# Seven block products of eight for w_proj_b, the b gates through DRAM, and weight sums copied by ScalarE

## The chip, the cores and the metric

The kernel runs on one core of a Trainium2 chip. A core has five engines, each with its own queue of instructions: TensorE (PE, matrix products into PSUM), VectorE (DVE), ScalarE (ACT), GpSimd (POOL) and SyncE (SP, which here only issues DMAs). PE, DVE and ACT do the work; any of SP, ACT and POOL can issue a transfer, and transfers that add onto their target are issued by POOL. The metric is the time of one execution on the device in microseconds (us).

## The reference

The program is one encoder layer in float32 over 512 tokens of width 1024: two mixers side by side, then cross-attention to 256 memory tokens, then a SwiGLU feed-forward part (FFN).

```python
n = rms_norm(x); proj = n @ w_in                # columns: xa, zu, zv, gate_a, gate_b
ya = s5_branch(xa)                              # scans in both directions, GELU, GLU with w_glu
yb = gelu(zu) * (mix(layer_norm(gelu(zv))) + bias)
merged = gate_a * (ya @ w_proj_a) + gate_b * (yb @ w_proj_b)
h = x + merged @ w_out
h = h + attention(rms_norm(h), rms_norm(mem))   # w_q, w_k, w_v, w_xo
h = h + (silu(m @ w_gate) * (m @ w_up)) @ w_down     # m = rms_norm(h)
out = rms_norm(h)
```

The change lies at `yb @ w_proj_b`, a product of 512x1024 by 1024x1024, and at the gate that multiplies it.

## The kernel before, in words

**Number format.** Each operand of a product is split into a high half (`whi`, a cast on ACT, line 85) and a low half (`wlo`, the difference on DVE, line 86). A product is then three matmuls: high with high, high with low, low with high (`mm3`, line 314).

**The weight stream.** All weights pass through one list, `plan`, in the order of use. An entry is a block of 128x1024 numbers (512 KB). `next_w` hands out the next pair of halves. It starts the loads of entries up to three ahead (`LOADS`, issued by SP, line 124, tile `wraw`, three buffers) and the splits of entries up to two ahead (`SPLITS`). A block of `feat` is used for 24 matmuls of 512 columns.

**Order.** The rows of `w_in` come first: zv (first half), xa, zv (second half), the a gates, zu, the b gates. The layer norm of zv (lines 903 to 913) and the mixing run beside the a gates. The a gates are written to DRAM (`gad`, line 947) and read back into `gat` (line 1027) for use in `pa_evac`.

**The S5 branch beside it.** The S5 branch is a generator, `s5_program`. After each block, `tick` lets it go on for a share of the block's time and runs what `later` has put off. It has a setup, kernels for four octets of groups (`s5_kernels`, tiles `e`, `pk`, `kd`, `tt`), inputs (`zh`), a scan of 62 steps of four small DVE operations (lines 798 to 801), and outputs for each octet (`s5_outputs`: copies `ss` on ACT, matmuls `py` at lines 822 to 824, GELU into `y`, a store to DRAM `yd` at line 832). `finish_side` traces what is left of it; then its memory pool (`s5`) is closed and the pool `merge` is opened in its place (lines 995 to 999), beginning with a small `pad`, then `ygt` and `yg_hi`/`yg_lo`, the operand of w_glu.

**Who orders the instructions.** Each engine runs its queue in order. The order within a queue is set when the program is built: a list scheduler takes, for each engine, the earliest instruction of the program that it thinks is ready. `keep_in_program_order` pins one instruction behind everything that was traced before it on its engine.

**The part around the change (lines 983 to 995).** For each 256 output columns, two blocks of the b gates run, their sigmoid goes into `part`, then two blocks of w_proj_b run on `yb`, and DVE multiplies the result by the gate in place:

```python
    for c0 in range(0, D, 256):
        feat(w_in, OFF_GB + c0, xn, KD, gb_evac)
        feat(w_proj_b, c0, yb, KD, pb_evac)
```

**Sums of w_down in DRAM.** The FFN already uses a scheme of seven block products instead of eight (Winograd's form of Strassen's algorithm): `product` (line 1254) runs 24 matmuls of 256 columns for one of seven products `q`, whose operands are blocks or sums of blocks. For w_down, four sums of blocks are prepared in DRAM (`dsum`): a copy from DRAM to DRAM issued by SP (`start`, line 223) and, three plan entries later, an add on top of it issued by POOL (`add`, line 226). There are 24 copies and 24 adds, from plan entry 14 to entry 86.

Of the kernel before, what the change touches and what calls it, by code (L numbers as in the profile page):

```python
# [9 lines left out]
F32 = mybir.dt.float32  # L10
# [42 lines left out]
def hybrid_layer_kernel(  # L53
# [147 lines left out]

    DOWN, CHUNKS = (1, 5, 2, 6, 3, 7, 4), 6
    DSRC = {1: (0, 0), 2: (1, 0), 3: (1, 1)}
    dsum = {q: dp.tile([P, NF // 2, 512], F32, name=f"dsum{q}") for q in (4, 5, 6, 7)}

# [6 lines left out]

    def plan_sums(first, step):


        more = {5: lambda c: down_block(0, 1, c), 7: lambda c: down_block(1, 1, c),
                6: lambda c: down_sum(5, c), 4: lambda c: down_sum(6, c)}  # L220

        def start(q, i, jc, c):
            tc.keep_in_program_order(nc.sync.dma_start(down_sum(q, c), down_block(i, jc, c)))

        def add(q, c):
            nc.gpsimd.dma_start(down_sum(q, c), more[q](c), accum_op=ALU.add)

        j = first
        for q, i, jc in ((5, 0, 0), (7, 0, 1), (6, 1, 1), (4, 1, 0)):
            for c in range(CHUNKS):  # L230
                plan[j][1].append((0, lambda x=(q, i, jc, c): start(*x)))
                plan[j + step][1].append((0, lambda x=(q, c): add(*x)))
                j += step

    def plan_down(w, make_tokens, entries):
        for q in DOWN:
            for c in range(CHUNKS):
                got = {}

                def load(q=q, c=c, got=got):  # L240
                    src = down_block(*DSRC[q], c) if q in DSRC else down_sum(q, c)
# [12 lines left out]
    plan_tok(w_in, OFF_V + 512, KD)  # L254
    first_copy = len(plan)
    for c0 in range(0, D, 256):
# [25 lines left out]
    plan_units(UNITS, down_plan)  # L282
    plan_sums(first_copy + 2, 3)
    used_w = [0]
# [193 lines left out]
    def slot(tag, shape, dt, name):  # L478
        return sp.tile(list(shape), dt, tag=tag, name=name)

    def token_slot(name, shift=0):

# [43 lines left out]
    def s5_setup():  # L526
# [23 lines left out]
        for nm, src in (("br", s5_b_re), ("bi", s5_b_im), ("cr", s5_c_re), ("ci", s5_c_im)):  # L550
# [10 lines left out]
            for c in range(C):  # L561
                nc.tensor.transpose(ps[:, c, :], rows[:, :, c], ident[:G, :G])
            t = s5p.tile([P, G, C], F32, name="raw_" + nm)
            A_.copy(t, ps.rearrange("p c g -> p g c"))
# [45 lines left out]
        for src in (pr, pi):  # L610
            pe = s5p.tile([P, G, Q], F32, name="pe%d" % len(st["pe"]))
            pw = s5p.tile([P, G, Q], F32, name="pw%d" % len(st["pw"]))
            A_.copy(pe[lo_], src[lo_, :, 0:Q])
# [353 lines left out]

    yb_hi = slot("E", (P, KD, T), F32R, "yb_hi")
    yb_lo = slot("D", (P, KD, T), F32R, "yb_lo")
    yb = (yb_hi, yb_lo)  # L970

# [10 lines left out]

    part = slot("A", (P, KD, T), F32, "part")

    def gb_evac(m, j, ps):
        nc.scalar.activation(part[:, m - OFF_GB // P, :], ps, AF.Sigmoid)

    def pb_evac(m, j, ps):
        nc.vector.tensor_tensor(part[:, m, :], ps, part[:, m, :], ALU.mult)
# [240 lines left out]

    K0, K1, T0, T1 = slice(0, 4), slice(4, 8), slice(0, 256), slice(256, 512)
    a11, a12, a21, a22 = full[:, K0, T0], full[:, K1, T0], full[:, K0, T1], full[:, K1, T1]
# [19 lines left out]
    fn_q = lambda ks, ts: (fn_hi[:, ks, ts], fn_lo[:, ks, ts])  # L1252
    ops = {1: fn_q(K0, T0), 2: fn_q(K1, T0), 7: fn_q(K0, T1), 4: fn_q(K1, T1)}

    def product(ps, u, q, start):

        hi, lo = next_w(u[0], u[1], q)
        for j in range(2):
            cs = slice(j * P, (j + 1) * P)
            for k in range(4):  # L1260
                a = (hi[:, k, cs], lo[:, k, cs])
                b = (ops[q][0][:, k, :], ops[q][1][:, k, :])
                for i, (x, y) in enumerate(((0, 0), (0, 1), (1, 0))):
                    nc.tensor.matmul(ps[:, j, :], a[x], b[y], start=start and j == k == i == 0,  # L1264
                                     stop=k == 3 and i == 2, skip_group_check=True)
        tick(2.7)

    def unit_bank(name):
        return bank(name).rearrange("p (j t) -> p j t", j=2)

# [86 lines left out]
    for i, u in enumerate(UNITS):  # L1357
# [9 lines left out]
        product(x, u, 6, False)  # L1367
        u2 = stp[0].tile([P, 2, 256], F32, tag="u2", name="u2", bufs=2)
        u3 = np_.tile([P, 2, 256], F32, tag="ev", name="u3", bufs=2)
# [152 lines left out]
```

## Time and profile before

| | us |
|---|---|
| median of three runs | 917.19 |
| lowest and highest run | 914.25, 920.67 |
| the profiled execution's own time | 915.85 |
| span of the profiled execution, first to last instruction | 914.1 |

The busy times add up the instructions of each engine. The chain that ended last goes back from the last instruction, at each step to what released it. In a row of a timeline stand the start, the length, the engine, the line and the tiles; in brackets how long the engine was idle before and what released it. `SPq` and `ACTq` are DMA issues on those engines' queues. A row of windows has the stretch, its length, the busy time and number of instructions of PE, PEld (weight loads), DVE, ACT and POOL, then the granted clock of PE as a share of full speed, the share of the DMA engines and GB/s. In a group stand the count, the busy time and the mean ns of one, and then the idle time before them.

### The profile page before, as it was taken

The numbers are of one execution on the slowest core, as the hardware profiler recorded it, in microseconds if no ns is written. First come the engines' busy times: TensorE is split into PE (matmuls) and PEld (weight loads), VectorE is DVE, ScalarE is ACT, GpSimd is POOL, SyncE is SP. The second block draws the span as 40 slices with busy tenths as digits, with TensorE's granted clock in tenths as the row PEclk, the third lists the DMA queues.
The fourth block names the chain that finished last, engine by engine and source line by source line (L and its number), as shares of the span: only waits on it lengthen the run. The fifth ranks groups of instructions, "written<-read, shape, count | busy, mean of one in ns | idle before, by whom it ended". The sixth has DMA issues, their size and how long they took to land.

```text
span 914.1 us, 14130 instructions
## 1 busy us (share of the span) xinstructions
PE 897.4 (98%) x5510; PEld 789.2 (86%) x5510; DVE 609.0 (67%) x991; ACT 458.7 (50%) x671; POOL 109.1 (12%) x163
## 2 busy tenths in 40 slices
PE   7999999999999999999999999999999999999996
PEld 6888888888888887789998888999999999888875
DVE  5596662888753235868545444786778777899875
ACT  5542995244374333445434433655554555655663
POOL 3003210000025301502000001000000000000000
PEclk8999999999999999999999999999999999999999
DMA  8445263675546655686895217415456463246572
GB/s 269 127 120 151 85 164 126 181 205 133 141 138 158 144 185 156 216 260 191 244 291 147 71 68 233 113 65 142 119 154 144 118 160 94 70 147 207 188 241 82
DMA packets 105987, 142.77 MB, mean 156 GB/s; under 512 B 13232, under 2 KB 73152, under 8 KB 105920
## 3 DMA queue, kind: packets, MB, share of 16 engines
q1 hardware_dynamic: 90688, 120.14, 40.9%
q0 software_dynamic: 12064, 19.37, 12.9%
q10 hardware_dynamic: 3168, 2.36, 0.9%
q8 instruction: 43, 0.70, 0.3%
q14 instruction: 24, 0.20, 0.1%
HBM read 135.06 MB, written 29.85 MB: 180 GB/s over the span
## 4 chain that ended last, share of the span: by engine, by line
PE 86%; ACT 4%; DVE 4%; DMA 3%; issue 2%; POOL 1%; POOLq 0%; SPq 0%; ACTq 0%; DVEq 0%
PE pf L314 31%; PE pt L314 14%; PE px L1264 12%; PE pq L1264 6%; PE dx L314 5%; PE dq L314 3%; PE pv L1264 3%; PE dv L314 2%; PE pk L714 2%; DVE wlo L86 1%; PE ptr L466 1%; PE po L314 1%; PE psc L314 1%; DMA wraw<-dsum 1%; ACT whi L85 1%
## 5 line engine op out<-in xcount | busy, mean ns | idle before, releaser
L86 DVE TENSOR_TENSOR wlo<-wraw,whi 128x1024 fp32r<-128x1024 f32 (+1 forms) x130 | 157.9, 1216 | 130.5 <-ACT whi L85 128.0
L85 ACT CAST whi<-wraw 128x1024 fp32r<-128x1024 f32 x132 | 135.4, 1028 | 174.5 <-PE pf L314 79.7
L314 PE MATMUL pf<-xn,whi 128*128 128x512 f32 x448 | 140.5, 392 | 0.0
L314 PEld LDWEIGHTS pf<-xn,whi 128*128 128x128 f32 x448 | 83.7, 188 | 17.3 <-issue 0.2
L314 PE MATMUL pf<-xn,wlo 128*128 128x512 f32 x224 | 87.6, 391 | 0.0
L1264 PE MATMUL px<-fn,whi 128*128 128x256 f32 x480 | 83.8, 277 | 0.0
L1264 PEld LDWEIGHTS px<-fn,whi 128*128 128x128 f32 x480 | 72.6, 188 | 0.3 <-ACT u L1377 0.2
L85 ACT CAST whi<-b 128x1024 fp32r<-128x1024 f32 x40 | 42.1, 1054 | 55.0 <-PE px L1264 26.8
L86 DVE TENSOR_TENSOR wlo<-b,whi 128x1024 fp32r<-128x1024 f32 x40 | 48.9, 1223 | 28.5 <-ACT whi L85 28.5
L1264 PE MATMUL px<-fn,wlo 128*128 128x256 f32 x240 | 66.3, 276 | 0.0
L314 PE MATMUL dx<-whi,s 128*128 128x512 f32 x170 | 53.9, 391 | 1.4 <-ACT whi L85 1.0
L1264 PE MATMUL pq<-s,whi 128*128 128x256 f32 x320 | 55.0, 276 | 0.0
L314 PEld LDWEIGHTS pf<-xn,wlo 128*128 128x128 f32 x224 | 42.1, 188 | 8.5
L1264 PEld LDWEIGHTS pq<-s,whi 128*128 128x128 f32 x320 | 48.3, 188 | 0.2
L86 DVE TENSOR_TENSOR wlo<-t,whi 128x1024 fp32r<-128x1024 f32 x30 | 36.7, 1224 | 15.9 <-ACT whi L85 15.9
L85 ACT CAST whi<-t 128x1024 fp32r<-128x1024 f32 x30 | 31.6, 1053 | 31.0 <-PE pv L1264 11.3
L314 PE MATMUL pt<-whi,xn 128*128 128x512 f32 x128 | 43.4, 412 | 1.8 <-ACT xn L85 1.5
L1264 PEld LDWEIGHTS px<-fn,wlo 128*128 128x128 f32 x240 | 45.1, 188 | 0.0
L1264 PE MATMUL pq<-s,wlo 128*128 128x256 f32 x160 | 44.2, 276 | 0.0
L314 PE MATMUL pf<-hn,whi 128*128 128x512 f32 (+1 forms) x160 | 41.8, 349 | 0.0
L314 PEld LDWEIGHTS dx<-whi,s 128*128 128x128 f32 x170 | 31.7, 188 | 8.5 <-ACT whi L85 1.2
L314 PE MATMUL dx<-wlo,s 128*128 128x512 f32 x85 | 33.3, 391 | 0.7 <-DVE wlo L86 0.7
(380 smaller groups left out, 2175.3 us busy)
## 6 DMA issues: line engine op xcount, KB each, us to landing
wraw<-in_w_in_dram SPq DMA_DIRECT2D x36, 512.0 KB, 3.8
dsum<-in_w_down_dram SPq DMA_DIRECT2D x20, 512.0 KB, 5.3
wraw<-dsum SPq DMA_DIRECT2D x20, 512.0 KB, 3.6
b<-in_w_gate_dram SPq DMA_DIRECT2D x15, 512.0 KB, 3.6
b<-in_w_up_dram SPq DMA_DIRECT2D x15, 512.0 KB, 3.6
wraw<-in_w_down_dram SPq DMA_DIRECT2D x15, 512.0 KB, 4.1
dsum<-in_w_down_dram POOLq DMA_DIRECT2D x10, 512.0 KB, 7.3
dsum<-dsum POOLq DMA_DIRECT2D x10, 512.0 KB, 6.1
```

The source lines that it names most:

```text
L85: nc.scalar.copy(dst_hi, src)
L86: (lo_eng or nc.vector).tensor_tensor(dst_lo, src, dst_hi.bitcast(F32), ALU.subtract)
L314: nc.tensor.matmul(ps, a[x], b[y], start=start and i == 0, stop=stop and i == 2, skip_group_check=free)
L466: nc.tensor.transpose(ps[:, j, :], src[:, k * P:(k + 1) * P], ident)
L714: nc.tensor.matmul(ps[32 * j:32 * j + 32, q, :], bd[i][:, g].rearrange("p d c -> p (d c)"), lc(es[i], g), start=(i == 0), stop=False, tile ...
L1264: nc.tensor.matmul(ps[:, j, :], a[x], b[y], start=start and j == k == i == 0, stop=k == 3 and i == 2, skip_group_check=True)
```

## The change

1. **w_proj_b as two units of seven products.** The eight entries of w_proj_b (192 matmuls of 512 columns) become 14 entries (`plan_pair`) of one product each, for two units `i` of 512 output columns, in the order of `PAIR`. All of the b gates now come before them. `run_pair` holds three PSUM banks for each unit, copies three of the results on ACT, and puts each quarter of the output through `put_part`, which multiplies by the gate on DVE.
2. **Sums of yb.** `quarter_sums` makes the operands of products 3, 5, 6 and 7 in eight steps on DVE and ACT, traced by `later` in the four blocks behind zu. They lie in slot A (`sy`), in the buffers of the norm gains (`s4y`) and in yb itself. The tiles of yb are moved by 16 numbers in their slots (`slot_moved`).
3. **Gates by way of DRAM.** The b gates go to `gbd` and come back by four loads into `gbt`, in slot B, which is xn's until the last b gate block. `part` moves from slot A to slot B.
4. **Weight sums.** `plan_sums` now makes both the sums of w_proj_b (`usum`, eight copies and adds, from 45 us of planned time in steps of 13) and those of w_down (from 200 us in steps of 18, so up to 632 us of planned time). ACT issues the copies, pinned to their place in the program; POOL still issues the adds.
5. **Buffers.** In the S5 pool, `raw_b` shares the buffer of `tt`, and the two `pw` become one tile whose buffer is used again for a temporary sum and `u2` of unit 0; a new buffer `u2` serves the other temporary and `u2` of unit 1. The FFN's `u2` moves to the buffer `xs`.

The diff, cut to its core:

```diff
+    PAIR = ((0, 1), (0, 5), (0, 2), (0, 6), (1, 1), (0, 7), (1, 2), (1, 5), (1, 6), (0, 4), (1, 7), (0, 3), (1, 4), (1, 3))
+    def plan_pair(w):
+        for i, q in PAIR:
+            src = usum[q][:, i] if q in MADE else unit_block(w, i, *RAW[q])
...
+            def load(src=src, got=got):
+                got["raw"] = wp.tile([P, kh, 256], F32, tag="raw", name="wraw", bufs=3)
+                nc.sync.dma_start(got["raw"], src)
+            plan.append(((w, i, q), [(LOADS, load)], lambda got=got: halves(got.pop("raw"))))
...
-            tc.keep_in_program_order(nc.sync.dma_start(down_sum(q, c), down_block(i, jc, c)))
+            tc.keep_in_program_order(nc.scalar.dma_start(dst(q, n), src(r, c, n)))
...
-        plan_feat(w_proj_b, c0, KD)
+    plan_pair(w_proj_b)
...
-    plan_sums(first_copy + 2, 3)
+    plan_sums(lambda q, n: 2 if n is None else usum[q][:, n],
+              lambda r, c, n: unit_block(w_proj_b, n, r, c), 45, 13)
+    plan_sums(lambda q, n: CHUNKS if n is None else down_sum(q, n), down_block, 200, 18)
...
-    part = slot("A", (P, KD, T), F32, "part")
+    def quarter_sums(hi, lo, s1, s2, s4, temps):
...
+        def one(i):
+            tt(i, a21[0], a22[0], ALU.subtract)
+            tt(i, temps[i], a21[1], ALU.add)
+            tt(i, temps[i], a22[1], ALU.subtract)
+            halve(i, s1)
...
+        return [lambda g=g, i=i: g(i) for g in (one, two, four, three) for i in range(2)]
+
+    sy = slot("A", (P, 2, 2, 4, 256), F32R, "sy")
+    s4y = [np_.tile([P, 4, 256], F32R, tag="gain", name="s4y", bufs=2) for _ in range(2)]
+    sums = [s5p.tile([P, 2, 256], F32, tag=tag, name="sum", bufs=1) for tag in ("pw", "u2")]
+    for i, fn_ in enumerate(quarter_sums(...)):
+        later(0.5 + 0.5 * i, fn_)
...
     def gb_evac(m, j, ps):
-        nc.scalar.activation(part[:, m - OFF_GB // P, :], ps, AF.Sigmoid)
-    def pb_evac(m, j, ps):
-        nc.vector.tensor_tensor(part[:, m, :], ps, part[:, m, :], ALU.mult)
+        z = np_.tile([P, T], F32, tag="ev", name="gbs", bufs=2)
+        nc.scalar.activation(z, ps, AF.Sigmoid)
+        nc.sync.dma_start(gbd[m - OFF_GB // P], z)
     for c0 in range(0, D, 256):
         feat(w_in, OFF_GB + c0, xn, KD, gb_evac)
-        feat(w_proj_b, c0, yb, KD, pb_evac)
+    pg = sp.tile([P, 2 * KD * T + 128], F32, tag="B", name="pg")[:, :2 * KD * T]
+    part, gbt = pg[:, 0], pg[:, 1]
+    for c in range(KD // 2):
+        nc.sync.dma_start(gbt[:, 2 * c:2 * c + 2], gbd[2 * c:2 * c + 2].rearrange("m p t -> p m t"))
+    def run_pair(w, put):
+        v, x, qb, u2, u3 = {}, {}, {}, {}, {}
+        for i, q in PAIR:
...
+            elif q == 6:
+                product(x[i], u, 6, False)
+                u2[i] = s5p.tile([P, 2, 256], F32, tag=("pw", "u2")[i], name="u2", bufs=1)
+                nc.scalar.copy(u2[i], x[i])
...
+            else:
+                product(qb[i], u, 3, False)
+                V.tensor_tensor(u2[i], qb[i], u2[i], ALU.subtract)
+                put(i, 1, T0, u2[i])
+    def put_part(i, f, ts, src):
+        m = slice(4 * i + 2 * f, 4 * i + 2 * f + 2)
+        V.tensor_tensor(part[:, m, ts], src, gbt[:, m, ts], ALU.mult)
+    run_pair(w_proj_b, put_part)
     finish_side()
     s5.close()
```

More of the change, by code (lines that the diff above doesn't have):

```diff
@@ L214, in down_sum, with plan_sums, at, start @@
         return dsum[q][:, 2 * c:min(2 * c + 2, NF // 2), :]
[L216 to L233, printed above, removed]
+    def plan_sums(dst, src, first, step):
+        ends = [0.0]
+        for key, _, _ in plan:
+            ends.append(ends[-1] + (5.4 if len(key) == 5 and key[0] is not w_k and key[0] is not w_v else 2.7))
+        def at(us, fn):
+            plan[next(j for j, e in enumerate(ends) if e >= us)][1].append((0, fn))
+        def start(q, r, c, n):
+            tc.keep_in_program_order(nc.scalar.dma_start(dst(q, n), src(r, c, n)))
+        def add(q, more, n):
+            nc.gpsimd.dma_start(dst(q, n), src(*more, n) if isinstance(more, tuple) else dst(more, n),
+                                accum_op=ALU.add)
+        for q, r, c, more in ((5, 0, 0, (0, 1)), (7, 0, 1, (1, 1)), (6, 1, 1, 5), (4, 1, 0, 6)):
+            for n in range(dst(q, None)):
+                at(first, lambda x=(q, r, c, n): start(*x))
+                at(first + step, lambda x=(q, more, n): add(*x))
+                first += step
     def plan_down(w, make_tokens, entries):
@@ L254, in hybrid_layer_kernel @@
     plan_tok(w_in, OFF_V + 512, KD)
-    first_copy = len(plan)
     for c0 in range(0, D, 256):
@@ L1252, in hybrid_layer_kernel @@
     fn_q = lambda ks, ts: (fn_hi[:, ks, ts], fn_lo[:, ks, ts])
[L1253 to L1269, printed above, removed]
+    ops.clear()
+    ops.update({1: fn_q(K0, T0), 2: fn_q(K1, T0), 7: fn_q(K0, T1), 4: fn_q(K1, T1)})
     def unit_start(u):
```

97 lines of the change are left out of this document (87 added, 10 removed).

## The prediction

> **What bounds the kernel now.** I read the page first: the busy shares, and the chain that ended last.
>
> ```profile
> PE 897.4 (98%) x5510; PEld 789.2 (86%) x5510; DVE 609.0 (67%) x991; ACT 458.7 (50%) x671; POOL 109.1 (12%) x163
> PE 86%; ACT 4%; DVE 4%; DMA 3%; issue 2%; POOL 1%; POOLq 0%; SPq 0%; ACTq 0%; DVEq 0%
> ```
>
> TensorE (PE) is the bound: nine tenths of the chain is matmul. The share is a mean, so I asked for the busy time of the stretches that the change touches (the layer norm; the scan beside the b gates; the rest of the b gates and w_proj_b in two pieces; the FFN).
>
> ```profile
> core 0: us, PE busy (x) PEld busy (x) DVE busy (x) ACT busy (x) POOL busy (x), PEclk, DMA share, GB/s
> 98.00:137.00 39.00, 38.03 (x232) 33.22 (x231) 25.17 (x32) 36.96 (x54) 6.93 (x7) 1.00 0.48 124
> 220.30:248.60 28.30, 28.30 (x126) 23.44 (x125) 23.75 (x96) 9.86 (x12) 1.17 (x1) 1.00 0.53 150
> 248.60:275.00 26.40, 26.40 (x188) 22.62 (x188) 13.29 (x13) 19.45 (x20) 5.94 (x14) 1.00 0.42 130
> 275.00:337.80 62.80, 62.80 (x393) 54.34 (x393) 18.00 (x19) 23.61 (x30) 19.84 (x41) 1.00 0.60 146
> 612.90:803.00 190.10, 189.08 (x1637) 187.47 (x1636) 146.91 (x146) 100.60 (x121) 10.21 (x8) 1.00 0.49 127
> ```
>
> PE is busy through all of 220.3 to 337.8, where w_proj_b runs. So each us of matmul taken out there is a us gained, as long as nothing new makes PE wait. The reader should see the second point too: in 220.3 to 248.6 VectorE (DVE) is busy 23.75 of 28.3 us, and in 98 to 137 ScalarE (ACT) 36.96 of 39. Those are the engines with little room.
>
> Next the chain in order of time gives matmul rates (start, length, matmuls), and the view of the tile yb_hi where w_proj_b stands.
>
> ```profile
> 176.91 77.13 PE pf L314 x340
> 434.45 10.55 PE pf L314 x88
> 615.59 8.16 PE px L1264 x72
> ```
> ```profile
> L314 PE MATMUL pf<-yb_hi,whi x64: 387/389/499, 231.2 to 337.1; 128*128 128x512 f32 x64
> L314 PE MATMUL pf<-yb_hi,wlo x64: 387/389/402, 231.7 to 337.6; 128*128 128x512 f32 x64
> ```
>
> A 512-column matmul takes 77.13/340 = 0.227 us. A 256-column one takes 8.16/72 = 0.113 us in the FFN products and 10.55/88 = 0.120 us in the k projection. w_proj_b now has 3 x 64 = 192 matmuls, interleaved with the b gates; the last starts at 337.6, and the first b gate block 10.9 us before 231.2, at 220.3.
>
> **Term 1, fewer matmuls.** Removed: 192 x 0.227 = 43.6 us. Added: 14 products x 24 = 336 at 256 columns, x 0.113 = 38.1 us. On the bound that is -5.5 us. If all ran at the k projection's rate (336 x 0.120 = 40.3) it is -3.3. I take the fast rate for the eight products on yb itself, which gets the 16-element shift that the FFN operand has, and the slow one for the six on sums that are unshifted: 144 x 0.0066 = +1.0. Sum -4.5, ends -5.5 and -3.3.
>
> **Term 2, a wait at the end of the stage.** How w_glu starts today:
>
> ```profile
> 323.41 0.22 PE py L823 x2
> 328.32 0.22 PE py L824 x2
> 328.55 17.80 PE pf L314 x78
> ```
> ```profile
> 329.20 1.77 SPq L832 DMA_DIRECT2D yd<-y  x4
> 332.79 1.77 SPq L1005 DMA_DIRECT2D ygt<-yd  x4
> ```
> ```profile
> 332.92 0.14 POOL L117 MEMSET pad<- 128x48 f32 x1 [20.02 <-DMA yd<-y]
> ```
> ```profile
> 335.71 1.14 ACT L85 CAST yg_hi<-ygt 128x512 fp32r<-128x512 f32 x2 [2.35 <-DMA ygt<-yd]
> ```
> ```profile
> 336.42 1.29 DVE L86 TENSOR_TENSOR yg_lo<-ygt,yg_hi 128x512 fp32r<-128x512 f32 x2 [0.47 <-ACT yg_hi L85]
> 340.49 0.68 DVE L86 TENSOR_TENSOR yg_lo<-ygt,yg_hi 128x512 fp32r<-128x512 f32 x1
> ```
>
> The memset of pad reads nothing of y, yet it waits 20 us for the store of y, and all four ygt loads start just then, though three of the octets lie in DRAM long before. So the merge pool takes the memory of the S5 pool as a whole, once its last tile is done with; today that is y. From there to the first yg_hi is 335.71 + 0.6 - 332.79 = 3.5 us, all of yg 8.4 us. It costs nothing, because the last w_proj_b matmuls (to 337.6) cover it.
>
> The change puts u2 of both units into the S5 pool, and u2 of unit 1 is read by the last put of the last product (1,3). So the pool opens only after PE has finished w_proj_b, and no matmul is left as cover: w_glu, w_proj_a and w_out all hang on yg. The path is two DVE operations and then the 3.5 us:
>
> ```profile
> L1390 DVE TENSOR_TENSOR u<-pq,u 128x512 f32<-128x512 f32 x10 | 6.8, 684 | 0.5 <-PE pq L1264 0.5
> L989 DVE TENSOR_TENSOR part<-pf,part 128x512 f32<-128x512 f32 x8 | 5.5, 691 | 9.3 <-PE pf L314 9.3
> ```
>
> 0.68 + 0.69 + 3.5 = 4.9 us as the low end with the wait; 1.4 + 8.4 = 9.8 if PE must have all of yg first. PE can start on the first pieces, so I take 5.9.
>
> **Term 3, the clock after that gap.** Windows of the start, the last matmul, and the end:
>
> ```profile
> 8.00:12.00 4.00, 1.90 (x10) 1.21 (x10) 2.28 (x5) 2.85 (x6) 2.41 (x2) 1.00 1.05 395
> 12.00:16.00 4.00, 3.18 (x10) 2.04 (x9) 3.93 (x4) 3.25 (x7) 2.86 (x2) 0.62 0.80 242
> 16.00:20.00 4.00, 3.79 (x12) 3.20 (x13) 3.53 (x9) 2.77 (x7) 0.55 (x1) 0.52 0.82 233
> 908.00:911.00 3.00, 0.00 (x0) 0.00 (x0) 0.87 (x2) 0.81 (x2) 0.52 (x1) 0.95 0.68 257
> ```
> ```profile
> 905.89 0.28 PE L314 MATMUL pcut<-whi,s 128*128 128x256 f32 x1
> ```
>
> After a stretch in which PE was busy 1.90 of 4 us, the granted clock (third column from the end) was 0.62 and 0.52 for two windows. After the last matmul it was still 0.95 in the third to sixth us. So a gap of 5.9 us probably costs half speed for some us after it: from 0 to about 3.4 us (half of the 7 us seen at the start). I take the middle, +1.8.
> The Trainium skill's page "TensorE: Matmul & The Clock Gate", section "Why this matters for your kernels", speaks against the change here: it allows no gap over about 3 us between bursts, since one idle window brings half speed, and by its busy window of about 3.4 us the loss would be an estimated 1.7 us. By it the sum below would be 0.1 lower.
>
> **Term 4, VectorE between 220 and 279.** The scan runs on DVE until 248.6. Added there are the quarter sums: 20 differences and 8 low halves of 128x512, 28 x 0.69 = 19.3 us. Weight splits go from 8 to 14:
>
> ```profile
> L86 DVE TENSOR_TENSOR wlo<-wraw,whi 128x1024 fp32r<-128x1024 f32 x16 | 19.6, 1225 | 41.6 <-ACT whi L85 40.4 <-DMA yd<-y 1.1
> L692 DVE TENSOR_TENSOR etmp<-raw_ci,pe 128x1024 f32<-128x1024 f32 x3 | 3.7, 1223 | 0.1
> ```
>
> PE reaches the first product after eight b gate blocks (192 x 0.227 = 43.6), two octets of py (5.1 each, 323.41 to 328.55) and one pk. pk: 337.8 - 220.3 = 117.5, less 16 blocks (87.1) and four py (20.6), leaves 9.8 for two. Sum 58.7, at 279. DVE's load until then: 23.75 less two part products (1.4), three more splits (3.7), quarter sums 19.3, two octets' e kernels (12 x 1.22 = 14.7): 60. That is over the 58.7 of PE, and a product eats a split each 2.7 us, half the time that a block gives now, with the splits only two ahead. Low end 0 (the second e waits behind the splits), high end 60 + 4.5 of idle as now - 58.7 = 6. I take +2, nearer the low end, since e of the second octet may move into the stage behind, where DVE is busy 18 of 62.8 us. What waits is the split, and behind it PE. The scan itself is earlier in the program than the sums. ACT's share (6 splits, 8 high halves, 6 PSUM copies) is hidden in its 19.45 of 26.4 and 23.61 of 62.8; without that cover it would be some 15 us.
>
> **Term 5, gates by way of DRAM.**
>
> ```profile
> gat<-gad SPq DMA_DIRECT2D x4, 512.0 KB, 7.3
> gad<-gas SPq DMA_DIRECT2D x8, 256.0 KB, 2.0
> ```
>
> The a gates go this way already. The four gbt loads need xn's slot, free at the last b gate matmul, and the fourth needs the last store (0.6 + 2.0 us later). They stand in SP's queue with the weight loads of products 3 and on behind them. The first put comes 3 x 2.7 = 8.2 us later, against 7.3 to land: hidden by a hair. Ends 0 and 3 (the queue held for the last store), I take +0.5. The 8 products with part on DVE become 8 puts of the same size.
>
> **Term 6, the copies.** 24 copies of w_down leave SP's queue and, with 8 new ones of w_proj_b, go to ACT's.
>
> ```profile
> L223 SPq DMA_DIRECT2D dsum<-in_w_down_dram x24: 536/558/1102, 122.5 to 513.6; - x24
> ```
> ```profile
> 127.58 1.22 POOL L226 DMA_DIRECT2D dsum<-in_w_down_dram  x1 [22.40 <-DMA dsum<-in_w_down_dram]
> ```
>
> Each issue costs the engine 0.56 us, 18 us of ACT in all, beside PE nearly everywhere. Where ACT is full (98 to 137) some three copies fall: 0 to +1.7 us. Against that, POOL's add held up the norm's factor r there for 22.4 us behind a late copy; if that ends, at most the 1.0 us of idle PE comes back. I take +0.8, since ACT is the nearer row. POOL's later adds meet the adds of the FFN weights; DMA is at 0.49 there and hides them. u2 of the FFN only changes its buffer: 0.
> The Trainium skill's page "DMA: Bandwidth & Descriptors", section "Issuing engines are not separate DMA queues", says that another issuing engine saves only the issue time on the sequencer. By it the move gives nothing, and the sum would be 0.8 lower if it cost nothing either.
>
> **Sum**, against the profiled execution's own 915.85 us (span 914.1): -4.5 + 5.9 + 1.8 + 2.0 + 0.5 + 0.8 = +6.5, so 922.3. The median of the three runs (917.19) is 1.3 above that execution; I give 922.5, near the sum.
>
> **The rivals.**
> - *The gap is covered* (faster): other matmuls fill it, or the pool's memory comes free earlier. For it: today's schedule shows no PE gap of that size. Against: nothing behind w_glu can start without it. Then terms 2 and 3 fall: 917.2 - 4.5 + 1.5 = 914; with no other cost 911.7. Chance 0.25.
> - *The S5 chain slips* (slower): if the quarter sums go ahead of the scan on DVE, py of the last octet, now ending at 328.5, comes up to 19 us later. From the end of py to w_glu are 9.3 us (328.5 to 337.8), and PE's work without a wait ends at 337.8 - 5.5 = 332; so it decides from py ending after 323. Its slack in the new order is five products less that, 13.6 - 9.3 = 4 us. A slip of 12 costs 8 more: about 930. For it: DVE's 60 in 58.7. Against: the scan stands first. Chance 0.17.
> - *SP's queue* stalls the products behind the gate loads, a few us more than term 5: 927. Chance 0.08.
>
> **How the numbers follow.** The forecast has 0.50, the covered gap 0.25, the S5 chain 0.17, SP 0.08. Within about 1% (908.0 to 926.4) a measurement of this kernel tells nothing apart. Below 908.0 lies a corner of the covered gap, 0.06. Above 926.4 lie the S5 chain and most of SP: 0.25 with the high ends of terms 2 and 4. The rest, 0.69, is within 1%. The range goes from 911 (the gap covered and no other cost) to 930 (the S5 chain); the forecast's own is 917 to 927.
>
> **What would show it.** Term 1: 336 matmuls of 256 columns on yb, sy and s4y at 0.113 or 0.120. Term 2: PE idle for 5 to 7 us ahead of the first yg matmul, with pad waiting for DVE's put and no longer for yd. Term 3: a granted clock under 1 right behind it. Term 4: gaps in front of the first products, released by wlo. Term 5: splits waiting for wraw. Term 6: POOL waits for copies much under today's. The forecast is wrong if PE runs through into w_glu, or if py of the last octet ends after the last product.

## The result, and the profile after

| | before | after |
|---|---|---|
| median of all runs, us | 918.93 (6 runs, 914.25 to 924.78) | 957.87 (6 runs, 948.96 to 964.71) |
| ratio, 95% interval | | 1.0397 [1.0331, 1.0463] |
| span of the profiled execution, us | 914.1 | 953.4 |

The change makes the kernel 39 us slower, where the prediction gave +6.5 and a range up to 930. First the page of the changed kernel: the busy times, and the chain that ended last by engine.

```profile
PE 908.0 (95%) x5654; PEld 806.6 (85%) x5654; DVE 633.5 (66%) x1029; ACT 465.6 (49%) x687; POOL 119.5 (13%) x171
PE 74%; DMA 9%; ACT 7%; DVE 4%; issue 3%; POOL 1%; SPq 0%; ACTq 0%; POOLq 0%; DVEq 0%
```

PE has only 10.6 us more of busy time, but it makes up 74% of the chain instead of 86%: now PE waits. To find where, I use one stage in every kernel below: from the last GELU of zu on ACT (just ahead of the b gates) to the first matmul of w_glu. Its row of windows in the kernel before:

```profile
221.20:337.80 116.60, 116.60 (x700) 99.65 (x699) 54.18 (x122) 52.02 (x61) 26.95 (x55) 1.00 0.54 143
```

and in the changed kernel:

```profile
222.10:369.80 147.70, 121.68 (x843) 112.16 (x841) 80.49 (x171) 60.30 (x77) 24.53 (x53) 0.87 0.60 174
```

The stage takes 31.1 us longer. PE is busy for 121.68 of 147.70 us, so it stands idle for 26.0 us, where it had no idle time; and the granted clock is 0.87 in the mean, which stretches the matmuls themselves. DVE's busy time rises from 54 to 80 us. The rest of the 39 us lies behind the stage: w_glu to w_xo takes 228.7 us instead of 224.3, and w_xo's last block to the first FFN matmul 24.7 instead of 20.9. These come up again below.

What PE waits for in the changed kernel (engine, line, what ended the wait; total us, times, longest):

```profile
PE py L862 <- DMA tt<-kd: 11.1, 1, 11.1
PE pf L346 <- DMA ygt<-yd: 8.4, 1, 8.4
```

Both are the end of the S5 chain: tt is the last octet's kernel matrix, ygt is S5's output. So the S5 branch is late. Its scan (62 steps, the first and last start):

```profile
L801 DVE TENSOR_TENSOR zh<-sa,sb x62: 210/225/228, 161.1 to 247.2; 128x64 f32<-128x64 f32 x62
```

and in the changed kernel:

```profile
L841 DVE TENSOR_TENSOR zh<-sa,sb x62: 210/224/227, 164.2 to 270.6; 128x64 f32<-128x64 f32 x62
```

Each instruction takes as long as before, but the last one comes 23.4 us later. DVE's timeline in the changed kernel shows why:

```profile
224.85 0.22 DVE L839 TENSOR_TENSOR sb<-zh,cb 128x64 f32<-128x64 f32 x1
224.99 0.68 DVE L86 TENSOR_TENSOR yb_lo<-zu,yb_hi 128x512 fp32r<-128x512 f32 x1
225.59 0.22 DVE L840 TENSOR_TENSOR sa<-sa,zh 128x64 f32<-128x64 f32 x1
225.73 0.68 DVE L1051 TENSOR_TENSOR sum<-yb_hi 128x512 f32<-128x512 f32 x1
226.33 0.68 DVE L86 TENSOR_TENSOR sy<-sum,sy 128x512 fp32r<-128x512 f32 x1
226.93 0.21 DVE L841 TENSOR_TENSOR zh<-sa,sb 128x64 f32<-128x64 f32 x1
227.07 0.68 DVE L1051 TENSOR_TENSOR sum<-sum,yb_lo 128x512 f32<-128x512 f32 x1
227.67 0.68 DVE L1051 TENSOR_TENSOR sum<-sum,yb_hi 128x512 f32<-128x512 f32 x1
228.27 0.21 DVE L838 TENSOR_TENSOR sa<-zh,ca 128x64 f32<-128x64 f32 x1
```

The reader should see the alternation. A scan step is four dependent operations (lines 838 to 841), each of which waits for the one before it. Into these short waits the scheduler has put other work, mostly one or two operations of the quarter sums each (the `yb_lo<-zu,yb_hi` here is the last split of zu), and each of those takes 0.68 us. All 28 operations of the sums start before the scan's last step.

Behind the scan the lateness grows. ACT then makes the inputs `ss` of two octets in one go, and the weight split has to wait for them:

```profile
270.44 1.05 ACT L85 CAST whi<-wraw 128x1024 fp32r<-128x1024 f32 x1 [1.35 <-PE pq L1034]
270.45 0.56 ACTq L254 DMA_DIRECT2D dsum<-in_w_down_dram  x1
271.39 1.13 ACT L856 COPY ss<-zh 64x504 f32<-64x504 f32 x1
...
279.13 1.06 ACT L857 COPY ss<-zh 64x504 f32<-64x504 f32 x1
280.21 1.04 ACT L85 CAST whi<-wraw 128x1024 fp32r<-128x1024 f32 x1
```

And at the end of the stage no work is left on PE (windows; the granted clock stands third from the end):

```profile
341.00:346.00 5.00, 0.00 (x0) 0.00 (x0) 0.00 (x0) 0.60 (x1) 1.49 (x3) 0.50 0.63 211
346.00:351.00 5.00, 0.03 (x1) 0.06 (x1) 0.00 (x0) 0.00 (x0) 2.69 (x6) 0.50 0.72 145
351.00:356.00 5.00, 5.00 (x24) 5.00 (x24) 0.00 (x0) 0.00 (x0) 0.00 (x0) 0.50 0.00 0
```

The last octet's py ends at 361 us (328.5 before), and its matmuls run at half clock. The merge pool's pad follows:

```profile
366.25 0.14 POOL L117 MEMSET pad<- 128x48 f32 x1 [17.56 <-DMA yd<-y]
```

It still waits for the store of y, as in the kernel before, and not for DVE's put of w_proj_b.

### The profile page after: what moved, and what is told of

Same layout as the page of the kernel before. It is cut to its first block, busy times and chain, and to the rows that moved or that the text cites. A ratio compares the mean times of both kernels' runs of the same rounds, so it can differ in the third digit from the quotient of the medians.

```text
span 953.4 us, 14562 instructions
## 1 busy us (share of the span) xinstructions
PE 908.0 (95%) x5654; PEld 806.6 (85%) x5654; DVE 633.5 (66%) x1029; ACT 465.6 (49%) x687; POOL 119.5 (13%) x171
## 4 chain that ended last, share of the span: by engine, by line
PE 74%; DMA 9%; ACT 7%; DVE 4%; issue 3%; POOL 1%; SPq 0%; ACTq 0%; POOLq 0%; DVEq 0%
PE pf L346 26%; PE px L1034 13%; PE pt L346 11%; PE pq L1034 6%; PE pv L1034 3%; PE dx L346 3%; DVE wlo L86 2%; ACT whi L85 2%; DMA b<-in_w_gate_dram 2%; PE dq L346 2%; PE dv L346 2%; DMA wraw<-dsum 1%; PE ptr L498 1%; DMA wraw<-in_s_w_glu_dram 1%; PE po L346 1%
## 5 line engine op out<-in xcount | busy, mean ns | idle before, releaser
L86 DVE TENSOR_TENSOR wlo<-wraw,whi 128x1024 fp32r<-128x1024 f32 (+1 forms) x136 | 164.9, 1215 | 103.8 <-ACT whi L85 101.0
L85 ACT CAST whi<-wraw 128x1024 fp32r<-128x1024 f32 x138 | 141.4, 1028 | 164.4 <-PE pf L346 61.3
L85 ACT CAST whi<-b 128x1024 fp32r<-128x1024 f32 x40 | 42.1, 1054 | 57.8 <-PE px L1034 26.6
L257 POOL DMA_DIRECT2D dsum<-in_w_down_dram x12 | 13.3, 1112 | 208.6 <-DMA dsum<-in_w_down_dram 177.1
```

The lines of the kernel that those rows point to most:

```text
L85: nc.scalar.copy(dst_hi, src)
L86: (lo_eng or nc.vector).tensor_tensor(dst_lo, src, dst_hi.bitcast(F32), ALU.subtract)
L257: nc.gpsimd.dma_start(dst(q, n), src(*more, n) if isinstance(more, tuple) else dst(more, n), accum_op=ALU.add)
```

## The experiments

My theory (sums first): the quarter sums on DVE hold up the scan, the S5 chain ends when w_proj_b has run out, and nothing covers it. The main rival (copies first): the weight-sum copies on ACT, and the adds behind them in POOL's queue, hold up the chain. Further suspects were the memory gate of the prediction's term 2, and the loads of x into h, which now run at 311 us because slot A is free early.

All results at a glance. The ratio is to runs of the kernel before that were taken beside it. The next columns are read from one profile of each kernel: the stage defined above, the start of the scan's last instruction, the start of the last py, and the stretch from w_xo's last block to the first FFN matmul.

| kernel | median, us | ratio [95%] | stage | scan | py | FFN opens |
|---|---|---|---|---|---|---|
| before | 918.9 | | 116.6 | 247.2 | 328.3 | 20.9 |
| before, a second profile | 922.4 | 1.0028 [0.9987, 1.0069] | 116.5 | 245.4 | 326.5 | 21.3 |
| after | 957.9 | 1.0397 [1.0331, 1.0463] | 147.7 | 270.6 | 361.0 | 24.7 |
| sums behind the scan | 937.8 | 1.0250 [1.0184, 1.0316] | 130.4 | 248.1 | 337.4 | 25.0 |
| no sums | 936.3 | 1.0201 [1.0156, 1.0245] | 122.0 | 246.6 | 323.3 | 27.5 |
| no sums, u2 out of the S5 pool | 921.7 | 1.0052 [1.0011, 1.0093] | 115.4 | 249.7 | 327.5 | 22.6 |
| after, w_down copies as before | 964.5 | 1.0494 [1.0429, 1.0559] | 154.6 | 268.3 | 364.7 | 24.6 |
| before, copies on ACT, step 18 | 927.3 | 1.0068 [1.0025, 1.0112] | 116.5 | 245.6 | 324.9 | 26.6 |
| before, copies on ACT, step 15 | 924.4 | 1.0038 [1.0004, 1.0073] | 116.5 | 245.9 | 326.9 | 22.3 |
| sums behind, h late | 932.7 | 1.0172 [1.0110, 1.0235] | 129.9 | 248.7 | 335.0 | 22.5 |
| the same, u2 out, ten sums on POOL | 933.6 | 1.0160 [1.0117, 1.0203] | 129.3 | 249.1 | 340.5 | 23.1 |
| sums late, other product order | 929.5 | 1.0106 [1.0055, 1.0156] | 125.9 | 249.4 | 336.7 | 24.1 |
| the same, copies at step 15 | 932.6 | 1.0148 [1.0104, 1.0192] | 117.5 | 246.8 | 328.3 | 28.9 |
| the same, copies from 345, step 9 | 933.7 | 1.0148 [1.0107, 1.0188] | 121.9 | 247.9 | 332.0 | 29.7 |

**1. The sums queued behind the scan.**

```diff
-        later(0.5 + 0.5 * i, fn_)
+        wait_sums.append(fn_)
+    later(0.5, lambda: behind_scan())
+    def behind_scan():
+        if st["step"][0] == NCH - 2:
+            with tc.issue_after(st["step"][1]):
+                for fn_ in wait_sums[:2]:
+                    fn_()
+            del wait_sums[:2]
+        if wait_sums:
+            later(0.5, behind_scan)
```

(`st["step"]` holds the number of the scan step traced last and its last instruction; `issue_after` only fixes the order in the queue, it adds no wait.)

> The changed kernel with one thing altered: VectorE's instructions of the quarter sums of yb are queued behind the scan's last step instead of between its steps. Theory (sums first): they stretch the scan from 248.6 to 270.8 us, and the S5 chain that starts from it ends 32 us later, after w_proj_b has run out, so that nothing covers it. Then here the scan ends at 245 to 252 us, w_glu starts before 345 us (369.8 in the changed kernel), and the time is 918 to 930 us. Rival (copies first): the weight-sum copies on ScalarE and the adds behind them on GpSimd's queue hold up the chain; then the scan ends on time but the last octet is still late, w_glu starts after 360 us, and the time stays above 945 us.

Measured: the scan ends at 248.1 us, and the stage falls from 147.7 to 130.4. DVE's timeline in this kernel has the scan step back at 0.8 us:

```profile
246.00 0.23 DVE L838 TENSOR_TENSOR sa<-zh,ca 128x64 f32<-128x64 f32 x1
246.14 0.22 DVE L839 TENSOR_TENSOR sb<-zh,cb 128x64 f32<-128x64 f32 x1
246.28 0.22 DVE L840 TENSOR_TENSOR sa<-sa,zh 128x64 f32<-128x64 f32 x1
246.53 0.22 DVE L841 TENSOR_TENSOR zh<-sa,sb 128x64 f32<-128x64 f32 x1
246.79 0.23 DVE L838 TENSOR_TENSOR sa<-zh,ca 128x64 f32<-128x64 f32 x1
```

So the order of DVE's queue alone is worth 17 us of the stage in these profiles, and 20 us between the medians (1.5% between the two ratios, some 13 us). The time, 937.8 us, lies between the two forecasts, and w_glu starts at 352 and not before 345 as expected: the same 19 us of sums now stand ahead of the next octets' kernels (`e`, lines 730 to 737), and py of the last octet still ends 9 us later than before.

**2. No sums at all.**

```diff
-        later(0.5 + 0.5 * i, fn_)
+        pass
...
+    ops.update({5: ops[4], 6: ops[7], 3: ops[2]})
```

> The changed kernel without the quarter sums: none of their instructions on VectorE and ScalarE are there, and products 5, 6 and 3 of each unit multiply quarters of yb itself, so w_proj_b's output is another one; everything else, the copies and the gates by way of DRAM too, is as in the changed kernel. Sums first: 913 to 924 us, scan ended by 250 us. Copies first: above 945 us, with the same waits for the tt and ygt loads as in the changed kernel.

Measured: the S5 chain is on time (py at 323.3 us) and the stage is 122.0, so the sums make 25.7 of the stage's 31.1 us. The time is 12 us above what I expected. By the profile three things make up most of it. One is a wait that takes the S5 chain's place:

```profile
220.10:342.10 122.00, 112.74 (x844) 103.54 (x842) 65.62 (x140) 58.96 (x71) 24.58 (x53) 0.99 0.68 202
```
```profile
336.22 0.14 POOL L117 MEMSET pad<- 128x48 f32 x1 [15.20 <-DVE pg L1140]
```
```profile
PE pf L346 <- ACT yg_hi L85: 7.5, 1, 7.5
```

Now pad waits for DVE's put into pg and comes 1.9 us after the last product's last matmul started (334.29), and PE waits 7.5 us for yg_hi. This is the prediction's term 2, in the place and of about the size that it had. The second is the FFN's pace (last section), nearly 7 us in this profile; the third is the opening of the FFN, 27.5 us instead of 20.9.

**3. The same, with unit 1's u2 in the norm pool.**

```diff
-                u2[i] = s5p.tile([P, 2, 256], F32, tag=("pw", "u2")[i], name="u2", bufs=1)
+                pool, tag = ((s5p, "pw"), (np_, "ev"))[i]
+                u2[i] = pool.tile([P, 2, 256], F32, tag=tag, name="u2", bufs=1 + i)
```

> The kernel without the quarter sums (products 5, 6 and 3 multiply quarters of yb itself, so w_proj_b's output is another one), and with unit 1's u2 put in a buffer of the norm pool instead of the S5 pool. Theory of the memory gate: without the sums the S5 chain is on time, and what opens the merge pool is the last reader of u2, just behind w_proj_b's last matmul; that made the 7.7 us gap of PE ahead of w_glu there (334.3 to 342.1 us). Here the gap is below 4 us and w_glu starts at 336 to 339 us. Rival: the gap comes from the landing of the ygt loads under the traffic of the h loads; then it stays above 6 us and w_glu starts after 341 us.

Measured: the stage is 115.4 us. Pad comes ahead of the last product (338.6 us), and PE goes straight into w_glu at 338.7.

```profile
334.43 0.14 POOL L117 MEMSET pad<- 128x48 f32 x1 [8.65 <-DVE pg L1141]
```

```profile
223.30:338.70 115.40, 113.13 (x843) 103.72 (x842) 62.47 (x136) 58.05 (x70) 24.53 (x53) 1.00 0.69 197
```

The gate theory holds: moving u2 is enough to close the gap. Traffic has a part in its size, though: behind the gate the ygt loads took 5.2 us to land (the median of the four), in the kernel before 2.8. Without any sum and without the gate the stage is 1.2 us shorter here than in the kernel before; PE is idle for 2.3 us of it, 1.1 of them behind a copy on ACT.

**4. Are the copies the cause?** The w_down copies issued by SP at their old places (`plan_old` is the `plan_sums` of the kernel before), all else as in the changed kernel:

```diff
-    plan_sums(lambda q, n: CHUNKS if n is None else down_sum(q, n), down_block, 200, 18)
+    plan_old(first_copy + 2, 3)
```

> The changed kernel with the w_down copies issued by SyncE at the places of the kernel before (from the first b-gate weights on, every third weight block); w_proj_b's own eight copies stay with ScalarE. Sums first: 950 to 960 us, as the changed kernel, with the scan ended at about 270 us. Copies first: below 935 us, and GpSimd's wait of 57 us for a copy is gone together with the wait of PE for tt.

Measured: 964.5 us, 4.5 above the range of "sums first", a stage of 154.6 us, and PE's wait for tt is longer still:

```profile
PE py L881 <- DMA tt<-kd: 19.8, 1, 19.8
```

"Copies first" falls; the two experiments without the sums, where all copies stayed on ACT and the S5 chain was on time, say the same. (The FFN ran at its slower pace in this profile.) The other way round, the kernel before with only the copies moved to ACT:

```diff
-    plan_sums(first_copy + 2, 3)
+    plan_sums(lambda q, n: CHUNKS if n is None else down_sum(q, n), down_block, 200, 18)
```

> The kernel before with one part of the change alone: its 24 w_down copies issued by ScalarE in program place, first at 200 us of the plan and every 18 us, with the adds one step behind. Sums first: 916 to 922 us, no PE gap above 2 us beside those of the kernel before. Copies first: 928 us or more, with waits of PE for the S5 chain between 250 and 345 us.

Its stage is untouched (116.5 us). Yet the time is 927.3 us, 0.7% up, [0.25, 1.1], more than the theory gave, and in the profile the place is the opening of the FFN. W_xo's last matmuls and the FFN's first, in the kernel before:

```profile
L314 PE MATMUL pt<-s,ot_hi x32: 389/389/476, 562.1 to 582.5; 128*128 128x512 f32 x32
L314 PE MATMUL pf<-fn,s x96: 279/279/365, 583.0 to 601.6; 128*128 128x256 f32 x96
```

and with the copies on ACT, step 18:

```profile
L319 PE MATMUL pt<-s,ot_hi x32: 387/389/775, 561.9 to 588.0; 128*128 128x512 f32 x32
L319 PE MATMUL pf<-fn,s x96: 279/279/365, 588.5 to 607.1; 128*128 128x256 f32 x96
```

The longest of these matmuls takes 775 instead of 476 ns: half clock, behind a gap of 3.6 us. There two copies issued on ACT (558.4 and 566.3 us) and two adds on POOL (571.0 and 581.7 us) run beside the loads that open the FFN; in the kernel before the last copy and add are issued at 514 and 519 us. By the profile's chain the way leads from one of these loads, which takes 15.6 us (10.8 in the kernel before), through the splits of its block on ACT and DVE to the norm behind them in DVE's queue, and PE waits for the norm's result xs:

```profile
562.74 15.60 DMA b<-in_w_gate_dram
```

With a step of 15 instead of 18 (`down_block, 200, 15`) one copy and one add fall there, and a second copy behind them at 583.0 us:

> The kernel before with the w_down copies issued by ScalarE in program place, first at 200 us and then every 15 us instead of 18 (927.3 us with 18, where the stretch that opens the FFN took 26.6 us against 20.9 and 21.2 in two profiles of the kernel before). If the late copies cost there: 917 to 922 us, and a stretch of 21 us. If it is ScalarE's issuing itself that costs, wherever it stands: 925 us or more.

Measured: 22.3 us at that place, and a time 0.4% up, [0.04, 0.7]. The place is as expected, the time is above it; the two intervals overlap, so the difference between the two steps is not settled by the times. Over all profiles the place took 20.9, 21.3 and 24.6 us where no copy or add ran beside these loads (the kernel before twice, and the w_down copies as before), 22.3 to 27.5 with one of each, and 26.6 to 29.7 with two or three of each. The counts go with the times, with a wide spread for one of each; no run varies this place alone.

**5. The early loads of x.** They were kept in program order on SP, behind the gat loads, on top of the sums behind the scan.

```diff
-        nc.sync.dma_start(h[:, t, :], x[t * P:(t + 1) * P, :])
+        tc.keep_in_program_order(nc.sync.dma_start(h[:, t, :], x[t * P:(t + 1) * P, :]))
```

> The kernel with the sums behind the scan (w_glu at 352.1 us, 937.8 us), and the four 512 KB loads of x into h kept in program order on SyncE, behind the gat loads, where in the changed kernel they run at 311 us because slot A is free early. If their traffic delays the end of the S5 chain and the ygt loads: w_glu starts at 344 to 349 us and the time falls by 3 to 8 us. If only VectorE's work decides: w_glu within 1.5 us of 352, the time within 2 us.

Measured: w_glu at 352.2 us, a stage of 129.9 against 130.4. There the forecast for "only VectorE's work decides" had put w_glu, but the trace shows another reason. The last py ends 2.4 us earlier than in experiment 1 and the last store of y lands at 339.4 us instead of 343.1, yet now the memory gate holds:

```profile
344.71 0.14 POOL L117 MEMSET pad<- 128x48 f32 x1 [16.30 <-DVE pg L1149]
```

So this run does not show that the loads are hidden: what the S5 chain gained, the gate of term 2 took. The time is 5 us lower, but the intervals overlap, and the profiles, 2.6 us apart, put most of the difference behind w_glu.

**6. Everything at once.** With ten of the 20 additions on POOL, the h loads late, and u2 out of the pool (`four` and `three` pass `nc.gpsimd`):

```diff
-            nc.vector.tensor_tensor(temps[i], f(x), f(y), op)
+            eng.tensor_tensor(temps[i], f(x), f(y), op)
```

> The sums behind the scan, the h loads late, u2 of unit 1 in the norm pool, and the additions of the last two of the four quarter sums (ten of 128x512) done by GpSimd instead of VectorE. If the cause is the S5 chain's delay on VectorE, the memory gate and the early loads, each repaired: w_glu starts at 335 to 342 us and the time is 914 to 926 us. If the weight-sum copies and adds cost more than these: above 930 us.

Measured: a stage of 129.3 us and 933.6 us, with the last py 5.5 us later than in experiment 5 and pad waiting for yd. This failed: the additions cost on POOL 2.3 to 4.5 times what they cost on DVE (681 ns), and POOL's queue also carries the S5 transfers tt and kd. That this is why py is late is argued, not tested. POOL's groups:

```profile
L1051 POOL TENSOR_TENSOR sum<-sum,yb_lo 128x512 f32<-128x512 f32 x6 | 10.6, 1774 | 0.1
L1051 POOL TENSOR_TENSOR sum<-sum,yb_hi 128x512 f32<-128x512 f32 x2 | 6.1, 3068 | 0.9 <-DVE sy L86 0.9
```

**7. The sums late, covered by products that need none.** Products 1 and 2 of both units come first, and the sums stand behind the scan and the third octet's kernels; h late and u2 out as above.

```diff
-    PAIR = ((0, 1), (0, 5), (0, 2), (0, 6), (1, 1), (0, 7), (1, 2), (1, 5), (1, 6), ...
+    PAIR = ((0, 1), (0, 2), (1, 1), (1, 2), (0, 5), (0, 6), (0, 7), (1, 5), (1, 6), ...
...
+    def form(n):
+        with tc.issue_after(st["last"]):
+            for fn_ in wait_sums[:n]:
+                fn_()
+        del wait_sums[:n]
...
+            form((2, 1, 1, 2, 1, 1)[n] if n < 6 else 0)
```

(`st["last"]` is the last instruction of the scan or of the third octet's kernels; `form` stands ahead of each of the first six products.)

> The h loads late and u2 of unit 1 in the norm pool, and the sums queued on VectorE behind the scan and the kernels of the third octet (27 us later than the scan's start), with the pair's products in another order: products 1 and 2 of both units, which need no sums, come first and cover them. If VectorE's place for the sums is what cost most, S5's last py stands near that of the kernel without sums (323 to 328 us) and w_glu starts at 336 to 342 us without a PE gap of over 4 us: 916 to 927 us, and if the FFN's products run at the faster of their two paces, 916 to 920. Rival: the sums come too late for products 5 and 6 and PE waits for them in the pair instead: gaps of 5 to 12 us at 275 to 290 us and 928 to 936 us.

Measured: 929.5 us, w_glu at 348.8, the last py at 336.7, and a stage of 125.9; the first three miss what I expected. PE does not wait for the sums in the pair (its largest gap there is 1.9 us at 286.7 us, for a copy on ACT), so that rival fails too; the S5 chain still ended 8 us late. The same kernel with the copies at a step of 15 (`down_block, 200, 15`):

> As the kernel with the sums late and the other order of products, and the 24 w_down copies at a step of 15 us of the plan instead of 18, so that the last copies and adds are over by about 570 us, ahead of the loads that open the FFN. If the late copies slow these loads, the stretch from w_xo's last block to the first FFN matmul goes from 22 to 27 us to 21 us and the time is 2 to 5 us below that kernel's; if not, within 1.5 us.

Here the stage is 117.5 us, the last py stands at 328.3 as in the kernel before, and pad waits for yd again:

```profile
333.83 0.14 POOL L117 MEMSET pad<- 128x48 f32 x1 [16.82 <-DMA yd<-y]
```
```profile
220.40:337.90 117.50, 114.24 (x844) 105.25 (x842) 80.52 (x166) 62.42 (x78) 24.57 (x53) 0.99 0.63 180
```

So with 80.5 us of DVE work the stage can be within 1 us of the kernel before. The time did not follow: the opening of the FFN took 28.9 us, against the 21 expected. The run did not do there what it was made for: the copies were not over by 570 us but went on until 710 us, and two copies (558.2 and 558.9 us) and two adds (565.0 and 569.2 us) ran beside the loads. (The FFN ran at its slower pace in both profiles.) Was it the copies that made the 8 us between these two stages? With `down_block, 345, 9`:

> As the kernel with the sums late and the other order of products (929.5 us with copies every 18 us from 200 us on; from zu's last evacuation to w_glu 125.9 us, against 117.5 us with a step of 15 us and 116.5 us in the kernel before), with all 24 w_down copies after the S5 stage: first at 345 us of the plan, every 9 us. If the copies and the adds, behind which GpSimd's S5 transfers stand in the queue, made the 8 us between those two kernels: 115 to 118 us here and w_glu at 334 to 339 us. If not: 122 us or more. The time follows what the denser copies cost in w_out to w_xo (224 to 228 us so far from w_glu to w_xo's last block): 917 to 926 us if that stays, above 930 us if they delay the weights there.

Measured: 121.9 us with no w_down copy in the stage (the first is issued at 464 us), where I expected 115 to 118. So the copies are not shown to be the cause. The time, 933.7 us, is above 930, though w_glu to w_xo took 224.4 us: three copies and three adds fell on the opening of the FFN, which took 29.7 us.

The traces split the 8.4 and 4.4 us by which these two stages are longer than the one with a step of 15. Counted from the stage's start, the last py comes 5.9 and 2.6 us later; why is open. Most of the rest is the landing of the ygt loads: 6.4 and 5.0 us, against 3.5 with a step of 15 and 2.8 in the kernel before (medians). Beside them run two loads that the change moved without anyone meaning to. The sums `s4y` lie in the buffers of the norm gains, and the last product reads them; so the gains of the next norms (`g_mem`, `g_x`, line 456), loaded at 150 and 178 us in the kernel before, come at the end of the pair: at 340 and 336 us in these two, just ahead of the ygt loads, and at 339 us, behind them, with a step of 15. No run tests this alone.

**8. The kernel before, once more.**

> The kernel before, unchanged, for a second profile. In the kernels without the sums and with the old copies, all 256-column products of the FFN ran at 118 ns instead of 113 ns, 6.8 us in sum, at the same addresses. If this pace belongs to the execution and not to the kernel, it can show here too: 1600 products' stretch of 176 or 182 us. The opening of the FFN (w_xo's last block to the first FFN matmul) took 20.9 us; if its 3 to 4 us in the changed kernels come from when loads happen to land, it is 1 us or more off here.

Measured: the stage is 116.5 us again, the FFN's products run at 113 ns again, and its opening takes 21.3 us, so neither difference that I asked about shows in this second profile. But w_glu to w_xo took 227.9 us, 3.6 more than in the first profile, with a gap of 2.6 us in w_out:

```profile
PE pt L314 <- ACT whi L85: 2.6, 1, 2.6
```

So the 4.4 us that the changed kernel had there say nothing about the change.

## Why the prediction was wrong

- **Term 1, fewer matmuls: right.** PE's busy time in the stage is 116.60 us before, and 112.74 and 113.13 in the two kernels without sums: -3.9 and -3.5, between the ends -5.5 and -3.3, less than the -4.5 taken. In the changed kernel the products on the sums ran at 0.117 to 0.120 us (0.120 taken); most of those on yb at 0.118 instead of 0.113.
- **Term 2, the memory gate: right in mechanism, and not what decided.** Without the sums, pad waits for the put and PE stands for 7.5 us (5.9 taken, ends 4.9 and 9.8); it goes when u2 leaves the pool. From PE's last product to the end of the put are 1.4 us, as taken; the way from pad to w_glu is 5.9 instead of 3.5, because the ygt loads land later. In the changed kernel itself the put is done at 336.0 us, the last store of y lands at 365.7, and pad waits for yd.
- **Term 3, the clock: right in size for one gap.** After the 7.5 us gap w_glu's 48 matmuls took 12.6 us instead of 10.6, +2.0 against +1.8. The estimate of 1.7 us, from the busy window of about 3.4 us that the Trainium skill's page "TensorE: Matmul & The Clock Gate" states in its Part 1, agrees as well. But the changed kernel has several gaps: its PE is busy 121.68 us for work that takes 112.7 at full clock, 9 us.
- **Term 4, VectorE: the step that failed.** It said "The scan itself is earlier in the program than the sums", and so counted the sums only as a delay of the weight splits (+2). The program order is as it said: in the built program 60 of the 62 scan steps stand ahead of the first sum. But a place in the program is not a place in the queue. The scheduler takes the earliest instruction that it thinks is *ready*. A scan step is rarely ready, since each operation waits for the last, and the sums always are. So 0.68 us operations went into the small holes, and a scan of 86.1 us became one of 106.4. The term's own row could have shown the limit: from 220.3 to 248.6 us DVE was idle for 4.5 us, so 19.3 us of sums put there had to lengthen the scan by about 15.
- **The rival "S5 chain slips" was the right one, with the wrong size and chance.** Its rule holds in the changed kernel: py's end plus 9.3 us gives w_glu's start (361.4 + 9.3 = 370.7; measured 369.8). It is no general rule: with the sums behind the scan the way took 14.4 us, and 16.9 with h late as well. The rival's slip, though, was 12 us, at most 19, and the measured one is 32.9. I bounded it by the duration of the sums (19.3 us), and the scan did stretch by about that (20.3 us; it also began 3.1 later). But some 9.5 us more came behind it, where I had counted nothing: the burst on ACT, the 11.1 us wait for tt, matmuls at half clock. It had 0.17 because "the scan stands first", the same false step.
- **Term 5, gates by way of DRAM: no wait of PE for them is seen.** SP's queue as a rival did not occur.
- **Term 6, the copies: the place was wrong.** It took +0.8 around 98 to 137 us, and dismissed the later ones ("DMA is at 0.49 there and hides them"). Alone, they cost 6.2 us [2.3, 10.3] (the ratio times 918), and the profile puts it at the opening of the FFN. The sign named for the term did not come either: POOL was to wait for copies much less than the 22.4 us it had named, and one wait, up to 277 us, is 57.4 us long.
- **The rival "The gap is covered"** did not occur, and its sum is not that of the terms: without terms 2 and 3 the others add 3.3 us and not 1.5, and 911.7 takes -5.5 for term 1.

Put together for the stage, taken out in this order and each read from one profile: sums 25.7, gate 6.6, all else -1.2; sum 31.1. In the changed kernel itself the gate costs nothing, because the S5 chain ends later still. With the wait at the gate gone and the S5 chain on time, the stage gains about 1 us on the kernel before, and no version tried beats the kernel before. The forecast named what would refute it, and that is what came: py of the last octet ends after the last product.

## What to carry to other kernels

A chain of small dependent operations on an in-order queue is slowed by any ready work that the scheduler may put between its links: when you add such work on the same engine, price it as a delay of the chain by its whole duration, wherever the program has it, or tie it behind the chain's last link. Then ask what hides the end of that chain; a change that shortens or moves the cover (here the b gates and w_proj_b behind one another) can turn each us of slip into a us of time and some more for the clock. Before you move a transfer "off the path", look at what else is loaded at its new time, not only where it was. And when new data borrow a buffer, ask which load waits for that buffer next.

## What the runs showed of the hardware

- **Two paces for the same matmuls.** The FFN's 256-column products ran at 113 ns in most profiles and at 118 ns throughout in five (no sums; w_down copies as before; and all three with sums late). The group's busy time in the kernel before:

```profile
L1264 PE MATMUL px<-fn,whi 128*128 128x256 f32 x480 | 83.8, 277 | 0.0
```

  and without the sums:

```profile
L1034 PE MATMUL px<-fn,whi 128*128 128x256 f32 x480 | 86.6, 279 | 0.0
```

  Over the FFN up to w_down this is 6.9 us (213.4 against 206.5). In the built programs the operands and weights of these matmuls lie at the same addresses in the changed kernel and in the one with the old copies, and the granted clock is 1.0 in both. Where the pace is fast, it becomes so at the first products behind w_up's 512-column block and stays. What decides is open. A comparison of kernels by one profile each has to allow for this.
- **Additions on POOL.** A 128x512 addition of two tiles took 1.6 to 3.1 us there (means of three groups; the profile's spans on POOL are rough), against 0.68 on DVE. The Trainium skill's page "GPSIMD Engine Reference", section "4.1 Engine selection", speaks of about twice DVE's time for two inputs; here it was 2.3 to 4.5 times.
- **A gap of 2 us can be enough to halve the clock.** In the changed kernel PE waited once for 2.0 us at the opening of the FFN, and the 3.4 us behind it ran at half clock (windows; the granted clock stands third from the end):

```profile
614.80:617.00 2.20, 0.40 (x2) 0.00 (x0) 0.94 (x3) 2.20 (x5) 0.56 (x1) 1.00 1.15 277
617.40:620.60 3.20, 3.20 (x11) 2.61 (x11) 2.72 (x4) 2.00 (x3) 0.00 (x0) 0.50 0.11 37
621.00:625.00 4.00, 4.00 (x27) 3.57 (x26) 3.42 (x7) 2.60 (x6) 0.07 (x1) 1.00 0.39 109
```

  The Trainium skill's page "TensorE: Matmul & The Clock Gate", section "Why this matters for your kernels", allows some 3 us; here the measurement decides. It is no rule the other way: in the kernel with the sums late, a gap of 2.7 us at the same place (589 us) was followed by full clock. Where the halving comes, it costs half of 3.4 us on top of the gap.
